# A residual made feature by feature early, turned to token order later, and read back in large loads

## The chip, the core and the metric

One core of one Trainium2 chip runs the whole program. The metric is the device time of one execution in microseconds. The engines are TensorE (PE; PEld is its weight load), VectorE (DVE), ScalarE (ACT), GpSimd (POOL) and SyncE (SP); here SP and POOL only issue DMAs. Each engine works through its own queue in order. On chip there are SBUF (128 partitions) and PSUM; `dram` tensors lie in device memory.

## What is computed

Two transformer-like blocks in a row, for 512 tokens of 2048 features. The first ends in a norm whose output x1 is both the input of the second and the residual of its first half:

```python
def first_block(x, p, ...):
    hn = rmsnorm(h, norm_gain[i])
    ...
    h = h + concatenate([ya, yb]) @ w_out[i]
    h = h + (p[i] @ w_ple[i]) * sigmoid(h @ w_ple_gate[i])
    return rmsnorm(h, final_gain)                       # x1

def second_block(x, c, positions, ...):                 # x is x1
    mod = silu(c) @ w_ada[l] + b_ada[l]
    sh_a, sc_a, gt_a, sh_f, sc_f, gt_f = split(mod, 6)
    h = rmsnorm_2(x, g_pre_attn[l]) * (1.0 + sc_a) + sh_a
    qa, ka, va, qb, kb, vb = split(h @ w_in[l], 6)
    ...                                                 # dilated and differential attention
    x = x + gt_a * rmsnorm_2(mix @ w_out[l], g_post_attn[l])
    h = rmsnorm_2(x, g_pre_ffn[l]) * (1.0 + sc_f) + sh_f
    f = (silu(h @ w_gate[l]) * (h @ w_up[l])) @ w_down[l]
    return x + gt_f * rmsnorm_2(f, g_post_ffn[l])
```

## The kernel before

**The matmuls.** Every large product is three matmuls on float32 split into a high and a low part: high by high, high by low, low by high. A weight piece (256 rows by 512 columns, 512 KB) is loaded by SP into `raw` (four buffers, up to six pieces ahead); up to three pieces ahead ScalarE copies the high half (`whi`) and VectorE subtracts it for the low half (`wlo`, L185). A gemm goes over the pieces; the order of TensorE's instructions is written by hand, while the queues of the other engines are put in order by a scheduler.

**Side work.** `side(steps, ticks, least=1)` (L120) gives a list of small steps to the program, and `tick()`, called once per k step of every gemm (12 matmuls in a full one), issues some of each list: `len(steps) / ticks`, but at least `least`. `finish` issues what is left of a list. `self.ada` is such side work: the adaLN product `silu(c) @ w_ada` on VectorE, tile after tile of `w_ada` (`wa`, 512 KB, SP), two multiply-adds (`ada`) for each.

**The pools.** The large pool `t4` has 30 buffers of 4 KB a partition; in it lie the split operands (16 tiles), the eight tiles `h2` of the first block's output, the attention's `qk` and `v`, the `wa` tiles, and later `mo`. The small pool `t2` has 8 buffers of 2 KB a partition for everything that passes by.

**x1.** `attention()` (L1203) starts with q and k of the first batch, then gives x1 as side work (L1238): 14 empty steps and 16 steps at half a step a tick. A step `x1(f)` (L1212) is, for a block of 128 features: on VectorE the product `x1 = h2 * final_gain * rxrow` (`rxrow` is the row of 1/rms, L1214; the trace prints the tile as `x`), on VectorE a transpose in blocks of 32 x 32 into `x1t` (L1217), and four DMAs on POOL into `x1d`, in device memory, in token order (L1219). The eight `h2` tiles stay until their last product. After q and k of a batch ScalarE copies the four PSUM tiles into fresh `qk` tiles (`project`, L1067).

**w_out2.** (L1267) The output projection runs with tokens on the partitions; its results go to `mo` tiles. The second half of the tokens of the later feature groups is computed while the first half is finished, and a first part of the feed-forward products (`up`) while the second half is. What finishes a half is `chain(hf)` (L1321), side work again: a load of the residual for three units ahead (`xr`, 256 KB, POOL, L1294), the root of the norm, then for eight units (4 groups of 512 features x 2 blocks of 128 tokens) the sum `mo = mo * root + xr` on VectorE (L1296), its square on ScalarE and a write to `x2d`, then the next load; then the second root, the normed tiles `xn`, their transposes on TensorE (`turn`, L1313) and the modulated operand `M` for the feed-forward products. `until` is a hook of a gemm that issues steps of the chain until the operand for its k is there.

Of the kernel before, what the change touches and what calls it, by code (L numbers as in the profile page):

```python
# [14 lines left out]
MUL, ADD, SUB, MAX = ALU.mult, ALU.add, ALU.subtract, ALU.max  # L15

P = 128
S = 512
D = 2048
KT = D // P  # L20
# [19 lines left out]
class Kernel:  # L40
# [1162 lines left out]
    def attention(self):  # L1203
        nc = self.nc
        cosA, sinA, cosB, sinB = self.tab[:4]
        self.mixd, self.x1d = self.dram("mixd", [D, S]), self.dram("x1d", [S, D])
        self.order = [b * 4 + h + (8 if kind == "b" else 0) for kind, b in self.BATCHES for h in range(4)]
        self.M = [None] * KT
        self.keep = False
        x, fg = self.H, self.cols["final_gain"]  # L1210

        def x1(f):  # L1212
            t = self.t2("x1")
            self.stt(t, self.h2[f], fg[:, f:f + 1], self.rxrow, MUL, MUL)  # L1214

            u = self.t2("x1t")
            nc.vector.transpose(u, t)  # L1217
            for b in range(4):
                nc.gpsimd.dma_start(self.x1d[:, f * P + b * 32:f * P + b * 32 + 32].rearrange("(c p) i -> p c i", p=32),  # L1219
                                  u[b * 32:b * 32 + 32, :].rearrange("p (c i) -> p c i", i=32))  # L1220

        def load(f):
            t = self.t2("ml")
            nc.sync.dma_start(t, self.mixd[f * P:(f + 1) * P, :])
            self.M[f] = self.pair("M")
            self.split(self.M[f], t)

        s = self.side(self.norm_steps(self.norm1(1), 1), 32)
        q, k = self.qk(), self.qk()
        for hf in range(2):  # L1230
            cs = slice(hf * 256, hf * 256 + 256)
            for o in (q, k):
                ps = self.gemm(x, half=hf)
                for i in range(4):
                    nc.scalar.copy(o[i][:, cs], ps[i][:, cs])
            if hf == 0:
                self.finish(s)
        self.side([None] * 14 + [lambda f=f: x1(f) for f in range(KT)], 60, 0)  # L1238
        self.adas = self.side(self.ada(12, 20), 165, 0)
        s = None  # L1240
        for n, (kind, b) in enumerate(self.BATCHES):
            t = (cosB, sinB, 32) if kind == "b" else (cosA, sinA, 64)
            if n == 3:
                break
            if n == 0:
                self.side(self.rope(q, *t) + self.rope(k, *t), 10)
            else:
                q, r = self.project(x, *t)
                self.side(r, 10)
                k, r = self.project(x, *t)  # L1250
                self.side(r, 10)
            v = self.values(x)
            if s:
                self.finish(s)
            s = self.side(self.attn_steps(kind, b, range(4), q, k, v), (47, 47, 31)[n])
        v = self.values(x)
        qk, r = self.project(x, *t)
        self.finish(s)
        self.keep = True
        self.side([None] * 2 + [lambda f=f: load(f) for f in self.order[:12]], 14)  # L1260
        s = self.side(r + self.attn_steps(kind, b, (0, 1), qk[:2], qk[2:], v), 16)
        qk, r = self.project(x, *t)
        self.finish(s)
        self.side(r + [None] * 6 + self.attn_steps(kind, b, (2, 3), [0, 0] + qk[:2], [0, 0] + qk[2:], v), 13)
        self.modding = self.H = None

    def w_out2(self):  # L1267

        nc, tc = self.nc, self.tc
# [6 lines left out]
        x = [[self.t4("mo", [P, 2, S]) for _ in range(2)] for _ in range(4)]  # L1276
# [5 lines left out]
        def evict(g, ps, b0):  # L1282
            for i, p in enumerate(ps):
                self.act(self.t2("sq"), p, AF.Square, accum_out=ss[:, 0, b0 + i, g:g + 1])
                self.tt(mo(b0 + i, g), p, corow[g], MUL)

        def root(n, b0, st):
            v = self.small("w2s", 2, 2)
            nc.vector.tensor_reduce(v, ss[:, n, b0:b0 + 2], axis=mybir.AxisListType.X, op=ADD)
            st[n] = self.rsq(v, 2)  # L1290

        def load(b, g, st):
            st[b, g] = self.t2("xr")
            nc.gpsimd.dma_start(st[b, g], self.x1d[b * P:(b + 1) * P, g * S:(g + 1) * S])  # L1294

        def add(b, g, st):  # L1296
            o = mo(b, g)
            self.stt(o, o, st[0][:, b % 2:b % 2 + 1], st.pop((b, g)), MUL, ADD)
            self.act(self.t2("sq"), o, AF.Square, accum_out=ss[:, 1, b, g:g + 1])
            nc.gpsimd.dma_start(self.x2d[b * P:(b + 1) * P, g * S:(g + 1) * S], o)  # L1300

        def normed(g, b0, st):
            st["n", g] = [self.t2("xn") for _ in range(2)]
            for i in range(2):
                self.ts(st["n", g][i], mo(b0 + i, g), st[1][:, i:i + 1], MUL)

        def turn(g, st):

            n = st.pop(("n", g))
            st["t"] = [self.aux("turn") for _ in range(2)]  # L1310
            for i in range(4):
                for b in range(2):
                    nc.tensor.transpose(st["t"][i // 2][:, (i % 2 * 2 + b) * P:(i % 2 * 2 + b + 1) * P],  # L1313
                                        n[b][:, i * P:i * P + P], self.ident)

        def mod(k, hf, st):
            i = k % 4
            self.mod_step(k, hf, st["t"][i // 2][:, i % 2 * 256:i % 2 * 256 + 256])
            st["done"] = k

        def chain(hf):  # L1321
            b0, st = 2 * hf, {"done": -1}
            units = [(b0 + i, g) for g in range(4) for i in range(2)]
            steps = [lambda: [load(*u, st) for u in units[:3]], None, lambda: root(0, b0, st), None]
            for n, u in enumerate(units):
                steps.append(lambda n=n, u=u: (add(*u, st), n < 5 and load(*units[n + 3], st)))
            steps += [None, lambda: root(1, b0, st), None, lambda: normed(0, b0, st), None, None, None]
            for g in range(4):
                steps += [lambda g=g: (turn(g, st), g < 3 and normed(g + 1, b0, st)), None]
                steps += [lambda k=k: mod(k, hf, st) for k in range(4 * g, 4 * g + 4)]  # L1330
            s = self.side(steps, len(steps))

            def until(k):
                while st["done"] < k:
                    f = s[0].pop(0)
                    if f:
                        f()
            return until

        for g in range(4):  # L1340
            evict(g, self.gemm(M, tok=True, half=None if g < 2 else 0), 0)
        self.finish(self.adas)
        F = self.M
        self.mod_begin(F, None, None, ("g_pre_ffn_2",), 3)
        self.us = [self.dram(f"us{n}", [256, S]) for n in range(self.NU)]

        def halves():
            for hf in range(2):
                hook = chain(hf)
                for n in range(2):  # L1350
                    if hf == 0:
                        evict(n + 2, self.gemm(M, tok=True, half=1), 2)
                    else:
                        self.up(n, self.gemm(F, half=0, hook=hook0 if n == 0 else None), slice(0, 256))
                hook0 = hook
            self.low.close()
            self.F, self.M = F, None
            if self.NS < self.NU:
                self.sp = self.ctx.enter_context(tc.tile_pool(name="sp", bufs=1, reuse_waits="tile"))
                self.C = [None] * 8  # L1360
                self.side([None] * 10 + [x for k in range(4) for x in (lambda k=k: self.sums(k), *[None] * 4)], 32)
            for n in range(2):
                self.up(n, self.gemm(F, half=1, hook=hook if n == 0 else None), slice(256, S))

        halves()
        for n in range(2, self.NS):
            hook = None
            if n == self.NS - 1 < self.NU - 1:
                hook = lambda k: self.sums(k // 2 + 1) if k in (6, 8, 10, 12) else None
            self.up(n, self.gemm(F, hook=hook))  # L1370

# [9 lines left out]
    def sums(self, k):  # L1381


        nc = self.nc
        A, B = self.F[k], self.F[k + 8]
        x, y = self.t2("sa"), self.t2("sb")
# [326 lines left out]
```

## Time and profile before

| | us |
|---|---|
| runs before: median of 3 (lowest, highest) | 3197.99 (3195.05, 3198.09) |
| the profiled execution's own time | 3195.01 |
| span of its profile | 3193.3 |
| TensorE matmuls busy | 3122.3 (98% of the span) |
| VectorE busy | 2357.3 (74%) |
| ScalarE busy | 1333.5 (42%) |
| GpSimd busy | 126.7 (4%) |

The mean clock that TensorE was granted in the profiled execution is 0.994 of full speed. The span is that of the instructions; the execution's time is 1.7 us more. TensorE's load of weights runs beside its matmuls and is not in the first number.

### The profile page before, as it was taken

To read this page: it belongs to the slowest core of one execution; us is meant where nothing else is said; L and a number is where in the kernel's file an instruction comes from. 1 tells how busy PE (TensorE), PEld (TensorE's weight loads), DVE (VectorE), ACT (ScalarE), POOL (GpSimd) and SP (SyncE) were. 2 spreads that over 40 slices of the span, in tenths; PEclk is the share of its full clock that TensorE was granted. 3 is DMA by queue.
4 is the path that set the end of the run, shared out by engine and by line. 5 is a ranking of instruction groups with operands and counts; after the bars stand their busy time and mean duration, and the time that the engine had idled before them with its cause. 6 is when DMAs were issued, how large, how long until landed. Compare 5 with 4: busy or idle time off the path is not lost. (4 is left out here: it accounts for less than half of the span.)

```text
span 3193.3 us, 50279 instructions
## 1 busy us (share of the span) xinstructions
PE 3122.3 (98%) x18484; PEld 2741.0 (86%) x18484; DVE 2357.3 (74%) x4638; ACT 1333.5 (42%) x2056; POOL 126.7 (4%) x217
## 2 busy tenths in 40 slices
PE   8999999999999899999899899999999999999998
PEld 7887878888899777788787899999999999888887
DVE  9787777866897587876745787888888888864445
ACT  6333443222466344433534653443334434333433
POOL 0010000000000021000001100000000000000000
PEclk9999999999999999999999999999999999999999
DMA  5763746755556365443426754444444445965664
GB/s 187 214 207 122 234 153 213 257 157 188 185 173 217 112 182 149 147 157 127 128 75 198 222 162 113 119 120 117 119 118 119 120 117 162 361 200 157 186 210 152
DMA packets 399624, 531.33 MB, mean 166 GB/s; under 512 B 43424, under 2 KB 222752, under 8 KB 399376
## 3 DMA queue, kind: packets, MB, share of 16 engines
q1 hardware_dynamic: 384448, 490.45, 49.0%
q0 software_dynamic: 10576, 29.70, 3.3%
q10 hardware_dynamic: 4352, 7.96, 0.7%
q8 instruction: 145, 2.38, 0.3%
q14 instruction: 103, 0.84, 0.1%
HBM read 491.34 MB, written 36.63 MB: 165 GB/s over the span
## 5 line engine op out<-in xcount | busy, mean ns | idle before, releaser
L185 DVE TENSOR_TENSOR wlo<-raw,whi 128x1024 fp32r<-128x1024 f32 (+1 forms) x655 | 756.2, 1160 | 478.9 <-ACT whi L261 390.4
L261 ACT CAST whi<-raw 128x1024 fp32r<-128x1024 f32 (+1 forms) x407 | 441.7, 1086 | 796.5 <-PE mm L315 344.0
L315 PE MATMUL mm<-H,whi 128*128 128x512 f32 (+1 forms) x2048 | 516.7, 344 | 12.9 <-ACT qk L1067 10.6
L1554 PE MATMUL mm<-whi,u 128*128 128x512 f32 x1344 | 415.0, 390 | 0.2 <-DVE u L185 0.2
L315 PEld LDWEIGHTS mm<-H,whi 128*128 128x128 f32 x2048 | 349.1, 192 | 57.6 <-ACT qk L1067 11.0
L315 PE MATMUL mm<-H,wlo 128*128 128x512 f32 (+1 forms) x1024 | 347.3, 339 | 1.5 <-DVE wlo L185 1.5
L315 PE MATMUL mm<-X,whi 128*128 128x512 f32 x1024 | 322.6, 396 | 8.4 <-ACT whi L261 6.7
L279 ACT CAST whi<-raw 128x1024 fp32r<-128x1024 f32 x152 | 159.7, 1051 | 400.5 <-issue 242.8
L194 DVE SCALAR_TENSOR_TENSOR ada<-wa,siluc,ada 128x512 f32<-128x512 f32 x360 | 268.8, 747 | 43.2 <-DMA wa<-in_w_ada_dram 38.2
L1554 PEld LDWEIGHTS mm<-whi,u 128*128 128x128 f32 x1344 | 251.7, 188 | 52.8 <-DVE u L185 0.6
L1554 PE MATMUL mm<-wlo,u 128*128 128x512 f32 x672 | 261.5, 389 | 0.0
L1444 PE MATMUL mm<-s,thi 128*128 128x256 f32 x1216 | 232.0, 283 | 0.0
L1444 PE MATMUL mm<-M,whi 128*128 128x256 f32 x1216 | 231.9, 283 | 0.0
L315 PEld LDWEIGHTS mm<-X,whi 128*128 128x128 f32 x1024 | 189.2, 189 | 48.8 <-ACT whi L261 6.7
L315 PEld LDWEIGHTS mm<-H,wlo 128*128 128x128 f32 x1024 | 195.9, 191 | 23.4 <-DVE wlo L185 1.7
L315 PE MATMUL mm<-X,wlo 128*128 128x512 f32 x512 | 201.3, 393 | 3.0 <-DVE wlo L185 3.0
L1444 PEld LDWEIGHTS mm<-M,whi 128*128 128x128 f32 x1216 | 189.8, 192 | 0.1
L1444 PEld LDWEIGHTS mm<-s,thi 128*128 128x128 f32 x1216 | 189.7, 192 | 0.0
L1444 PE MATMUL mm<-M,wlo 128*128 128x256 f32 x608 | 172.1, 283 | 0.0
L1444 PE MATMUL mm<-s,tlo 128*128 128x256 f32 x608 | 172.1, 283 | 0.0
L313 PE MATMUL mm<-whi,H 128*128 128x512 f32 x512 | 162.6, 399 | 0.0
L313 PE MATMUL mm<-whi,M 128*128 128x512 f32 x512 | 160.8, 395 | 1.3 <-ACT qk L1067 1.3
(390 smaller groups left out, 6016.3 us busy)
## 6 DMA issues: line engine op xcount, KB each, us to landing
wa<-in_w_ada_dram SPq DMA_DIRECT2D x192, 512.0 KB, 6.0
raw<-in_w_in_dram SPq DMA_DIRECT2D x111, 512.0 KB, 3.9
raw<-in_w_down_dram SPq DMA_DIRECT2D x88, 512.0 KB, 4.2
raw<-in_w_out_dram SPq DMA_DIRECT2D x80, 512.0 KB, 4.2
ur<-us SPq DMA_DIRECT2D x140, 256.0 KB, 4.6
raw<-in_w_in_dram SPq DMA_DIRECT2D x130, 256.0 KB, 3.1
raw<-in_w_ple_gate_dram SPq DMA_DIRECT2D x48, 512.0 KB, 4.0
raw<-in_w_gate_dram SPq DMA_DIRECT2D x152, 128.0 KB, 2.1
```

What stands on the lines that cost most here:

```text
L185: self.nc.vector.tensor_tensor(o, x, y, op=op)
L194: self.nc.vector.scalar_tensor_tensor(o, x, s, y, op0=op0, op1=op1)
L261: nc.scalar.copy(h, r)
L279: nc.scalar.copy(hv, v)
L313: nc.tensor.matmul(ps[i], x[k][:, xi, c], wt[:, a, :], **fl)
L315: nc.tensor.matmul(ps[i][:, cs], wt[:, a, c], x[k][:, xi, cs], **fl)
L1444: nc.tensor.matmul(ps[j][:, s], wt[:, s, slot], self.C[k][j][xi], start=(k == 0 and s == 0 and i == 0), stop=(k == 7 and s == 1 and i == 2))
L1554: nc.tensor.matmul(ps[b], u[a][:, xi, b * P:(b + 1) * P], wt[:, a, :], start=(n == a == j == 0), stop=(n == NU - 1 and a == 1 and j == 2))
```

## The change

Three pieces of code are changed. In `attention`, `x1(f)` makes the product only and has SP write it to a new tensor `x1f` in device memory, features by tokens; the 16 steps come at one a tick, with no empty steps ahead. A second list, `self.x1s`, does the rest later: after 44 empty steps, for each of the 16 blocks `back(f)` (SP loads the block from `x1f` into a small tile), one empty step, `turn(f)` (the transpose and the four DMAs on POOL as before) and four empty steps, one step a tick. It is finished after the first feature group of `w_out2`. In `w_out2` the loads of a unit are replaced by `load(b0)`: four loads of 512 KB (two feature groups each) into the large pool, issued for the first half ahead of `mod_begin`, and for the second half at the end of the first half's eight sums. The chain's lists keep their length.

```diff
+        self.x1f = self.dram("x1f", [D, S])
+        turned = {}
+
         def x1(f):
             t = self.t2("x1")
             self.stt(t, self.h2[f], fg[:, f:f + 1], self.rxrow, MUL, MUL)
+            nc.sync.dma_start(self.x1f[f * P:(f + 1) * P, :], t)
+
+        def back(f):
+            turned[f] = self.t2("x1")
+            nc.sync.dma_start(turned[f], self.x1f[f * P:(f + 1) * P, :])
+
+        def turn(f):
 
             u = self.t2("x1t")
-            nc.vector.transpose(u, t)
+            nc.vector.transpose(u, turned.pop(f))
...
-        self.side([None] * 14 + [lambda f=f: x1(f) for f in range(KT)], 60, 0)
+        self.side([lambda f=f: x1(f) for f in range(KT)], 40)
+        self.x1s = self.side([None] * 44 + [x for f in range(KT) for x in (lambda f=f: back(f), None, lambda f=f: turn(f),
+                                                                          *[None] * 4)], 156)
...
-        def load(b, g, st):
-            st[b, g] = self.t2("xr")
-            nc.gpsimd.dma_start(st[b, g], self.x1d[b * P:(b + 1) * P, g * S:(g + 1) * S])
+        x1s = {}
+
+        def load(b0):
+            x1 = x1s[b0] = [[self.t4("xr", [P, 2, S]) for _ in range(2)] for _ in range(2)]
+            for g in range(2):
+                for b in range(2):
+                    tc.keep_in_program_order(
+                        nc.gpsimd.dma_start(x1[b][g].rearrange("p g n -> p (g n)"),
+                                            self.x1d[(b0 + b) * P:(b0 + b + 1) * P, g * 1024:g * 1024 + 1024]))
 
         def add(b, g, st):
             o = mo(b, g)
-            self.stt(o, o, st[0][:, b % 2:b % 2 + 1], st.pop((b, g)), MUL, ADD)
+            self.stt(o, o, st[0][:, b % 2:b % 2 + 1], x1s[b & 2][b % 2][g // 2][:, g % 2], MUL, ADD)
...
-            steps = [lambda: [load(*u, st) for u in units[:3]], None, lambda: root(0, b0, st), None]
-            for n, u in enumerate(units):
-                steps.append(lambda n=n, u=u: (add(*u, st), n < 5 and load(*units[n + 3], st)))
-            steps += [None, lambda: root(1, b0, st), None, lambda: normed(0, b0, st), None, None, None]
+            steps = [None, None, lambda: root(0, b0, st), None] + [lambda u=u: add(*u, st) for u in units]
+            steps += [lambda: hf == 0 and load(2), lambda: root(1, b0, st), None, lambda: normed(0, b0, st), None, None, None]
...
             evict(g, self.gemm(M, tok=True, half=None if g < 2 else 0), 0)
+            if g == 0:
+                self.finish(self.x1s)
         self.finish(self.adas)
+        load(0)
```

The change moves instructions on the engines that a scheduler puts in order; TensorE's order stays as it is. Three places, in each the queue before and the queue now. The numbers behind a name tell one tile from another.

ScalarE's queue in the attention, at the copies of a projection's results into `qk`, with what each instruction waits for (DMAHW and DMASW are DMAs of the hardware and the software queues). Before:

```order
L258 CAST whi_10185<-raw_9946 128x512 [waits DMAHW7_49,DMAHW6_49,PE_49]
L258 CAST whi_10185<-raw_9946 128x512
L1149 COPY pT_10170<-turn_10166 128x384 [waits PE_49]
L1067 COPY qk_10172<-mm_9593 128x512 [waits DMAHW5_49,DMAHW1_49,DVE_49]
L1067 COPY qk_10172<-mm_9594 128x512
L1067 COPY qk_10173<-mm_9595 128x512 [waits DMAHW6_49,DMAHW2_49,DVE_49]
L1067 COPY qk_10173<-mm_9596 128x512
```

Now:

```order
L197 ACTIVATE oq_10139,ss_9904<-mix_10136 128x128 [waits DVE_49]
L1067 COPY qk_10205<-mm_9642 128x512 [waits PE_49]
L197 ACTIVATE p_10169,den_9903<-p_10169,m_10170 128x512 [waits DVE_49,Activation_49]
L197 ACTIVATE p_10174,d_1684_10162<-p_10174,m_10175 128x512 [waits DVE_49,Activation_49]
L1067 COPY qk_10205<-mm_9643 128x512 [waits PE_49]
L1067 COPY qk_10206<-mm_9644 128x512 [waits PE_49]
L1149 COPY pT_10203<-turn_10199 128x384 [waits PE_49,Activation_49]
L1067 COPY qk_10206<-mm_9645 128x512
```

The copies waited for two loads and for VectorE beside what is done already; now they wait for TensorE, and two softmax steps (`p`) stand between them.

SP's queue in the attention, around the first load back of x1. Before:

```order
L227 DMA raw_10603<-in_w_in_dram 128x2x512
L227 DMA raw_10675<-in_w_in_dram 128x2x512
L940 DMA wa_10792<-in_w_ada_dram 128x2x512
L227 DMA raw_10750<-in_w_in_dram 128x2x512
L227 DMA raw_10840<-in_w_in_dram 128x2x512
L940 DMA wa_10978<-in_w_ada_dram 128x2x512
L940 DMA wa_11063<-in_w_ada_dram 128x2x512
```

Now:

```order
L227 DMA raw_10596<-in_w_in_dram 128x2x512
L227 DMA raw_10660<-in_w_in_dram 128x2x512
L1222 DMA x_1798_10678<-x1f 128x512
L227 DMA raw_10729<-in_w_in_dram 128x2x512
L227 DMA raw_10817<-in_w_in_dram 128x2x512
L940 DMA wa_10941<-in_w_ada_dram 128x2x512
L940 DMA wa_11024<-in_w_ada_dram 128x2x512
L227 DMA raw_10891<-in_w_in_dram 128x2x512
```

A load from `x1f` stands between the weight loads; the other 15 follow further on in the same way, among `raw`, `wa` and `mixd` transfers.

VectorE's queue in `w_out2`, at the sums of the first half. Before:

```order
L194 SCALAR_TENSOR_TENSOR mo_14559<-mo_14559,rsy_15745,xr_15717 128x512
L194 SCALAR_TENSOR_TENSOR mo_14561<-mo_14561,rsy_15745,xr_15719 128x512
L194 SCALAR_TENSOR_TENSOR mo_14559<-mo_14559,rsy_15745,xr_15721 128x512
L185 TENSOR_TENSOR wlo_15799<-raw_15705,whi_15798 128x1024
L194 SCALAR_TENSOR_TENSOR mo_14561<-mo_14561,rsy_15745,xr_15782 128x512
L185 TENSOR_TENSOR wlo_15829<-raw_15729,whi_15828 128x1024
L194 SCALAR_TENSOR_TENSOR mo_14560<-mo_14560,rsy_15745,xr_15794 128x512
L185 TENSOR_TENSOR wlo_15857<-raw_15766,whi_15856 128x1024
L194 SCALAR_TENSOR_TENSOR mo_14562<-mo_14562,rsy_15745,xr_15812 128x512
L194 SCALAR_TENSOR_TENSOR mo_14560<-mo_14560,rsy_15745,xr_15824 128x512
L185 TENSOR_TENSOR wlo_15883<-raw_15796,whi_15882 128x1024
L194 SCALAR_TENSOR_TENSOR mo_14562<-mo_14562,rsy_15745,xr_15842 128x512
```

Now:

```order
L194 SCALAR_TENSOR_TENSOR mo_14608<-mo_14608,rsy_15796,xr_15727 128x512
L194 SCALAR_TENSOR_TENSOR mo_14610<-mo_14610,rsy_15796,xr_15729 128x512
L194 SCALAR_TENSOR_TENSOR mo_14608<-mo_14608,rsy_15796,xr_15727 128x512
L185 TENSOR_TENSOR wlo_15846<-raw_15762,whi_15845 128x1024
L194 SCALAR_TENSOR_TENSOR mo_14610<-mo_14610,rsy_15796,xr_15729 128x512
L194 SCALAR_TENSOR_TENSOR mo_14609<-mo_14609,rsy_15796,xr_15728 128x512
L185 TENSOR_TENSOR wlo_15872<-raw_15780,whi_15871 128x1024
L194 SCALAR_TENSOR_TENSOR mo_14611<-mo_14611,rsy_15796,xr_15730 128x512
L194 SCALAR_TENSOR_TENSOR mo_14609<-mo_14609,rsy_15796,xr_15728 128x512
L194 SCALAR_TENSOR_TENSOR mo_14611<-mo_14611,rsy_15796,xr_15730 128x512
```

Eight sums before used eight tiles `xr` of one load each, with four `wlo` among them; now two sums share a load, and two `wlo` stand among them.

## Rows read from the trace of the kernel before

**Rows 1.** The page, part 1: engines, busy us (share), instructions.

```profile
PE 3122.3 (98%) x18484; PEld 2741.0 (86%) x18484; DVE 2357.3 (74%) x4638; ACT 1333.5 (42%) x2056; POOL 126.7 (4%) x217
```

**Rows 2.** Windows of 40 us: stretch, length, busy us (x instructions) per engine, PEclk, DMA share, GB/s.

```profile
1040.00:1080.00 40.00, 40.00 (x191) 31.50 (x189) 18.02 (x57) 17.12 (x41) 0.00 (x0) 1.00 0.28 89
1080.00:1120.00 40.00, 29.39 (x152) 22.73 (x148) 28.67 (x95) 13.38 (x38) 5.84 (x9) 0.92 0.50 147
1160.00:1200.00 40.00, 38.90 (x197) 30.39 (x196) 36.05 (x115) 19.08 (x45) 15.22 (x24) 1.00 0.70 199
1200.00:1240.00 40.00, 37.99 (x182) 30.98 (x181) 32.90 (x74) 19.65 (x36) 10.50 (x17) 1.00 0.54 144
1800.00:1840.00 40.00, 32.84 (x252) 31.86 (x251) 25.59 (x52) 24.50 (x41) 3.79 (x7) 0.91 0.61 194
```

**Rows 3.** Waits of TensorE, 1000 to 1280 us: us in total, times, longest.

```profile
PE mm L315 <- ACT qk L1067: 10.6, 1, 10.6
PE logits L1100 <- ACT oq L197: 2.9, 1, 2.9
```

**Rows 4.** Timeline at 1110 to 1120: start, length, instruction, [idle before <-releaser].

```profile
1110.47 0.75 DVE L194 SCALAR_TENSOR_TENSOR ada<-wa,siluc,ada 128x512 f32<-128x512 f32 x1 [2.98 <-DMA wa<-in_w_ada_dram]
...
1116.64 0.74 DVE L194 SCALAR_TENSOR_TENSOR x<-h,vecs,rxrow 128x512 f32<-128x512 f32 x1
...
1117.97 0.70 DVE L1217 STREAM_TRANSPOSE x1t<-x 128x512 f32<-128x512 f32 x1
...
1119.34 1.07 ACT L1067 COPY qk<-mm 128x512 f32<-128x512 f32 x2 [9.00 <-DVE ada L194]
...
1119.97 1.22 PE L315 MATMUL mm<-H,whi 128*128 128x512 f32 x2 [10.61 <-ACT qk L1067]
```

**Rows 5.** Windows of 4 us, columns as in rows 2.

```profile
1118.00:1122.00 4.00, 2.03 (x5) 1.64 (x6) 2.84 (x6) 2.15 (x4) 2.56 (x4) 0.50 0.84 266
1122.00:1126.00 4.00, 4.00 (x18) 3.29 (x17) 1.80 (x3) 0.37 (x2) 0.04 (x1) 0.78 0.40 74
1150.00:1154.00 4.00, 4.00 (x10) 3.13 (x10) 2.89 (x9) 0.00 (x0) 0.00 (x0) 0.50 0.54 150
1816.00:1820.00 4.00, 3.74 (x17) 3.74 (x18) 0.93 (x3) 0.35 (x1) 1.08 (x2) 0.50 0.59 197
```

**Rows 6.** Waits of TensorE, 1720 to 1830 us, in `w_out2`.

```profile
PE mm L313 <- DVE wlo L185: 3.2, 2, 2.4
PE mm L315 <- ACT u L197: 2.4, 1, 2.4
PE mm L315 <- DVE u L185: 2.3, 1, 2.3
PE mm L315 <- DVE M L185: 1.6, 1, 1.6
PE turn L1313 <- DVE xn L189: 1.6, 1, 1.6
PE mm L315 <- DVE wlo L185: 0.8, 1, 0.8
```

**Rows 7.** The tile `xr`: the sums that read it, and their waits (us, times).

```profile
L194 DVE SCALAR_TENSOR_TENSOR mo<-mo,rsy,xr x16: 743/750/753, 1738.7 to 1807.2; 128x512 f32<-128x512 f32 x16
...
  DMA xr<-x1d: 15.6, 8
```

**Rows 8.** DMA issues: operation, count, KB each, median us to landing.

```profile
xr<-x1d POOLq DMA_DIRECT2D x16, 256.0 KB, 5.7
...
x<-x2d SPq DMA_DIRECT2D x8, 512.0 KB, 6.1
...
ml<-mixd SPq DMA_DIRECT2D x12, 256.0 KB, 4.3
```

**Rows 9.** The tile `x1t`: duration ns min/median/max, first and last start.

```profile
L1217 DVE STREAM_TRANSPOSE x1t<-x x16: 695/706/714, 1096.1 to 1223.1; 128x512 f32<-128x512 f32 x16
```

**Rows 10.** Timeline of ScalarE ahead of `u`.

```profile
1810.97 1.28 ACT L197 ACT_TABLE_LOAD   x1
```

More of the change, by code (lines that the diff above doesn't have):

```diff
@@ L1214, in x1 @@
             self.stt(t, self.h2[f], fg[:, f:f + 1], self.rxrow, MUL, MUL)
+            nc.sync.dma_start(self.x1f[f * P:(f + 1) * P, :], t)
[3 more added lines that the diff above has]
+        def turn(f):
             u = self.t2("x1t")
-            nc.vector.transpose(u, t)
+            nc.vector.transpose(u, turned.pop(f))
             for b in range(4):
                 nc.gpsimd.dma_start(self.x1d[:, f * P + b * 32:f * P + b * 32 + 32].rearrange("(c p) i -> p c i", p=32),
-                                  u[b * 32:b * 32 + 32, :].rearrange("p (c i) -> p c i", i=32))
+                                    u[b * 32:b * 32 + 32, :].rearrange("p (c i) -> p c i", i=32))
         def load(f):
```

## Prediction

> **What bounds the kernel now.** The first view is the busy shares of the engines: TensorE's matmuls fill 3122.3 us of the span of 3193.3 [rows 1], so 71 us are left in which TensorE stands, and the order of its instructions does not change. An edit elsewhere can win only from those 71 us and from matmuls that run at the lower of the two clock levels. The second view, windows of 40 us, shows where both lie around the code that changes: between 1080 and 1120 us TensorE stands 10.6 us at a granted clock of 0.92, between 1800 and 1840 it stands 7.2 us at 0.91, while in the stretch just ahead, 1040 to 1080, it never stands and VectorE is busy for 18.02 us of 40 [rows 2]. The third view, who waited for whom on TensorE, names the causes. In the attention one wait for ScalarE's copy `qk` (L1067) takes 10.6 us and one for `oq` 2.9 [rows 3]; in `w_out2` seven waits take 11.9 us [rows 6].
>
> The timeline explains the large one. ScalarE's copy into the new `qk` tile starts only at 1119.34, after 9.00 us of idleness that an `ada` step of VectorE ended, and TensorE goes on 0.6 us later [rows 4]. Why would a copy out of PSUM wait for an `ada` step? The `qk` tile takes a buffer of the large pool (30 buffers) which a `wa` tile held, and VectorE reads that tile last; the order of the kernel before writes the same wait on the copy. VectorE has a queue there: it had waited 2.98 us for the load of `wa` and then runs adaLN steps, x1's product and x1's transpose, 0.7 us each, in program order [rows 4]. The pool is tight because the eight tiles `h2` (the first block's output) live until x1 is made of them, and x1 comes one of 16 feature blocks per two ticks, transposed from 1096 to 1223 us [rows 9].
>
> The other place, in `w_out2`, is simpler: VectorE's sums `mo` stand 15.6 us in 8 waits for the loads of `xr` [rows 7], which are issued three units ahead and take 5.7 us to land [rows 8]. VectorE is in order, so the weight halves `wlo`, the normed tile `xn`, `M` and `u` behind those sums are late, and TensorE waits for each of them [rows 6].
>
> **What the change does, and its price.**
>
> *The large stall.* x1's 16 products (0.74 us each [rows 4]) now run one per tick, ahead of the second batch; in VectorE's order all stand 70 rows or more ahead of the place where the first stood before, in the stretch in which VectorE was busy less than half the time. 16 x 0.74 = 12 us more there against 22 us of idle [rows 2]: I cost it at nothing, under TensorE's cover; without that cover it would be 12 us. With them the eight `h2` buffers come free, and `wa` tiles go there. In the order of the changed kernel the copies into `qk` wait for TensorE alone. So the 10.6 us go, and with them the slow matmuls behind: TensorE restarted at a granted clock of 0.50, the lower of its levels of 1.2 and 2.4 GHz (2.03 us of work up to 1122, worth 1.0) and 0.78 (4.00 us, worth 0.9) [rows 5], against 1.00 elsewhere. Together 12.5 us.
>
> *The rest of that stretch.* The wait of 2.9 us for `oq` [rows 3] and the 4.00 us at half clock that follow (worth 2.0) [rows 5] come from ScalarE's own queue and VectorE's lateness together; the transposes (16 x 706 ns, 11.3 us) leave VectorE in that stretch, where it was busiest [rows 9]. I take half of 4.9: 2.5 us. Between 1160 and 1240 TensorE stands 3.1 us in small waits [rows 2]; half again: 1.5. Bounds of the two together: 0 and 8.0.
>
> *The sums of `w_out2`.* Four loads of 512 KB stand ahead of each half. A load of that size took 6.1 us to land (`x<-x2d`), one of 256 KB 5.7 [rows 8]. The first four are issued right after the block's last adaLN piece, at about the time of the first `xr` loads before; the other four follow the last sum of the first half. The sums run from 1738.7 to 1807.2 in two groups [rows 7], so both sets have far longer than 6 us to land, and no sum waits for them. In the first half TensorE then loses its waits for `wlo` (3.2) and `xn` (1.6): 4.8. In the second half those for `wlo` (0.8) and `M` (1.6) go: 2.4. The two at the handover, `u` of ScalarE and of VectorE (2.4 and 2.3), come of the same lag: about half of the 15.6 us [rows 7] fall into this half. But a new table load of 1.28 us stands ahead of `u` on ScalarE whatever VectorE does [rows 10], so I leave 1.5 of the 4.7 and take 3.2. The matmuls behind ran 3.74 us at 0.50 [rows 5]: 1.9. Sum 12.3; bounds 4.8 (the first half alone) and 13.8 (all of it).
>
> Against joining loads speaks a rule of the Trainium skill, Perfetto Trace Analysis, section DMA Optimizations: splitting a DMA may let some of the work start sooner. By it the first sum of a half would stand until a whole 512 KB had landed. That would cost at most the 0.4 us between the two landings, and nothing where the load is early; the sum stays as it is.
>
> *New traffic.* SP issues 16 more writes (to `x1f`) and 16 more loads (back into SBUF), each 256 KB, between the weight loads. The nearest row: a load of that size and kind from the same queue (`ml`) landed in 4.3 us [rows 8]. Each write waits for a product that VectorE runs ahead of the `wlo` that frees the next weight buffer, so the loads behind it are not held. Each load back stands two ticks ahead of its transpose. A tick is 12 matmuls; 191 in 40.00 us make that 2.5 us [rows 2], so there are 5.0 us for 4.3. That is a thin margin, and SP's queue adds to it where a `raw` or `wa` load waits for its buffer. When the transpose waits, so do `wlo` and the attention's steps behind it on VectorE. In `w_out2`, 15.6 us of such waiting on VectorE cost TensorE 9.5 (all its waits for VectorE there, 3.2 + 2.3 + 1.6 + 1.6 + 0.8): 0.61 for one [rows 6, 7]. I choose half of the 16 loads 0.4 us late, a tenth of a landing: 8 x 0.4 x 0.61 = 2 us. Ends: 0, and 42 (16 x 4.3 x 0.61, a whole landing each time). I am near the low end because weight halves are made three pieces ahead, six ticks or 15 us.
>
> A second rule speaks against the round trip: the Trainium skill, DMA: Bandwidth & Descriptors, section Issuing engines are not separate DMA queues, says that transfers of every engine share the same 16 DMA engines. By it the 8.4 MB could slow `wa` and `raw`; the trace has a share of 0.28 to 0.70 in these stretches [rows 2], so there is room in each on average, and I add no term.
>
> POOL issues the same 64 transposed pieces, only spread out, and 8 loads for 16; nobody waits for its queue.
>
> **Sum.** 12.5 + 2.5 + 1.5 + 12.3 - 2 = 26.8, about 27 us. The profiled execution took 3195.0, so 3168 on its scale. The median of the three runs is 3198.0, 3 us above it; the forecast of a median is **3171 us**, 0.8% less.
>
> **Rivals.**
>
> 1. *The loads of `w_out2` don't become early.* The four tiles are the large pool's, and that pool is full there: 16 tiles of the second block's operand, 8 `mo`, 4 + 4 `xr` are 32 against 30. The second half's loads must wait for the first half's tiles. For: the count. Against: they are issued behind the last sum of the first half anyway, when its tiles are free, and the second half's first sum is a whole gemm away. It gives 4.8 instead of 12.3: 19 us, 3179. Chance 0.12.
>
> 2. *The large stall only moves.* Eight `ada` steps still stand close together in VectorE's order at that place, and if their loads are as late as before (2.98 us [rows 4]) the softmax steps behind them are late, and TensorE stands at the next `logits` or `turn` instead. For: the waits named `oq` and `turn` follow close behind already [rows 3]. Against: with eight buffers more, `wa` loads are issued earlier. The 12.5, 2.5 and 1.5 shrink to about 2: 12 us in all, 3186. Chance 0.13.
>
> 3. *Slower: the loads back stop VectorE.* SP works in order; a load back that queues behind a weight load waiting for its buffer lands after its transpose is due, VectorE stands, `wlo` slips, TensorE waits and restarts at half clock. The gains are 26.8 + 2 = 28.8; at 0.61 they are used up when VectorE stands 47 us in all, 2.9 per load; at 4.3 per load the result is 28.8 - 42 = 13 us slower, 3211. For: the margin of 0.7 us. Against: three pieces of lead, and VectorE was busy 18 to 36 of 40 us in the stretches shown [rows 2], so it can catch up between two loads. Chance 0.07. The shared engines of the second rule would act through this same wait.
>
> 4. *Nothing comes of it.* The order's waits are not the times: another tile of the large pool may hold `qk` back, and the sums may stand for ScalarE instead. Gains and costs cancel: 3195 to 3201. Chance 0.08.
>
> The forecast's own case has 0.60.
>
> **How the numbers follow.** Best case of the bounds: 12.5 + 8.0 + 13.8 = 34, 3164, and a run as fast as the fastest of before lies 3 lower, 3161. I set the range from 3158 to 3189, which takes in rivals 1 and 2 and leaves out 3, 4 and some tails, under 2 in 10. A measurement of this kernel can tell about 0.2%, 6.4 us, from no change. Faster by more than that: the forecast's case, rival 1 and most of rival 2, 0.84. Same 0.09, slower 0.07.
>
> **What would show it.** In the profile after: no wait of TensorE for `qk` L1067 above 1 us near 1110, the granted clock 1.00 there; VectorE busier from 1040 to 1080; no wait of `mo` for `xr`, and TensorE's waits in `w_out2` down from 11.9 to about 2; landings of `x<-x1f` near 4.3 us and few waits of `x1t` for them. Wrong: a new wait for `oq`, `logits` or `turn` of 5 us or more at 1110 to 1130 (rival 2), `x1t` waiting 2.9 us or more for each load (rival 3), `mo` still waiting for `xr` in the second half (rival 1).

## The result, and the profile after

| | us |
|---|---|
| changed kernel: median of 4 (lowest, highest) | 3159.61 (3158.48, 3162.62) |
| kernel before, 4 runs | 3196.52 (3193.18, 3198.09) |
| ratio, 95% interval | 0.9887 (0.987 to 0.9905) |
| profiled executions: before, after | 3195.01, 3162.62 |

The medians differ by 36.9 us; 3171 had been forecast, with a range of 3158 to 3189. The forecast was on the right side and inside the range, and it asked for too little: 27 us against 37. The gain is also above the 34 us that the prediction gave as its best case; the time lies inside the range only because the lower end was set 6 us below that case.

The page of the changed kernel begins:

```profile
span 3160.9 us, 50349 instructions
PE 3115.3 (99%) x18484; PEld 2737.2 (87%) x18484; DVE 2355.8 (75%) x4638; ACT 1333.5 (42%) x2056; POOL 121.9 (4%) x209
```

TensorE is busy 7 us less than before [rows 1], with the same instructions, and the span is 32.4 us shorter, so most of the gain is time in which it stood. The windows that answer to [rows 2] (same columns):

```profile
1040.00:1080.00 40.00, 39.24 (x183) 30.77 (x182) 23.46 (x62) 15.18 (x36) 0.00 (x0) 1.00 0.49 161
1080.00:1120.00 40.00, 40.00 (x206) 31.43 (x204) 22.92 (x92) 18.55 (x51) 0.00 (x0) 1.00 0.37 119
1160.00:1200.00 40.00, 39.90 (x205) 31.94 (x205) 30.06 (x87) 25.76 (x52) 5.21 (x8) 1.00 0.56 179
1200.00:1240.00 40.00, 39.02 (x184) 30.82 (x184) 29.20 (x80) 12.79 (x26) 5.18 (x8) 1.00 0.65 200
1800.00:1840.00 40.00, 40.00 (x336) 39.81 (x335) 30.01 (x49) 28.09 (x47) 2.17 (x4) 1.00 0.56 175
```

The two stretches that stood out are full: 1080 to 1120 went from 29.39 to 40.00, 1800 to 1840 from 32.84 to 40.00, both at a granted clock of 1.00. All of TensorE's waits of 0.3 us or more from 1040 to 1240 us and from 1690 to 1850 us are now:

```profile
PE turn L1147 <- DVE p L194: 1.0, 2, 0.6
PE logits L1100 <- DVE m L1108: 0.8, 2, 0.6
PE logits L1100 <- ACT oq L197: 0.3, 1, 0.3
```

```profile
PE mm L315 <- ACT u L197: 2.4, 1, 2.4
```

The waits for `qk` (10.6) and of 2.9 for `oq` [rows 3] are gone or down to 0.3, and of the seven waits in `w_out2` [rows 6] one is left, ScalarE's `u`. ScalarE's copies into `qk`, which answer to [rows 4], no longer wait for VectorE:

```profile
1110.90 0.59 ACT L1067 COPY qk<-mm 128x512 f32<-128x512 f32 x1 [1.94 <-PE mm L315]
...
1112.91 1.05 ACT L1067 COPY qk<-mm 128x512 f32<-128x512 f32 x2
```

GpSimd's queue shows the loads of `xr`. The first four leave some 170 us ahead of the first sum (1719.99), the other four right after the first half's last write and 34 us ahead of the second half's first sum (1765.35); no sum waits for one of them:

```profile
1548.97 0.57 POOL L1311 DMA_DIRECT2D xr<-x1d  x1 [18.41 <-ACT oq L197]
1553.07 0.55 POOL L1311 DMA_DIRECT2D xr<-x1d  x1 [3.53 <-ACT M L200]
1555.77 0.53 POOL L1311 DMA_DIRECT2D xr<-x1d  x1 [2.14 <-PE mm L315]
1558.50 0.53 POOL L1311 DMA_DIRECT2D xr<-x1d  x1 [2.20 <-PE mm L315]
...
1721.03 1.87 POOL L1318 DMA_DIRECT2D x2d<-mo  x3 [162.00 <-DVE mo L194]
...
1728.55 1.74 POOL L1311 DMA_DIRECT2D xr<-x1d  x3
1730.51 0.53 POOL L1311 DMA_DIRECT2D xr<-x1d  x1 [0.21 <-issue]
```

The transposes stand where the timing of the second list puts them, a load back lands in 3.5 us, and a load of 512 KB in 6.7 (columns as in [rows 8, 9]):

```profile
L1227 DVE STREAM_TRANSPOSE x1t<-x x16: 700/704/714, 1166.3 to 1527.0; 128x512 f32<-128x512 f32 x16
```

```profile
x<-x1f SPq DMA_DIRECT2D x16, 256.0 KB, 3.5
...
xr<-x1d POOLq DMA_DIRECT2D x8, 512.0 KB, 6.7
```

**Where the time went.** TensorE's order is the same in both kernels, so the start of the same instruction can be compared in the two traces. The table gives that difference at a few of them, and the step since the one above:

| instruction of TensorE | before | after | difference | step |
|---|---|---|---|---|
| first `fin` after 570 | 573.29 | 575.29 | +2.00 | +2.00 |
| first `logits` after 1050 | 1054.99 | 1058.53 | +3.54 | +1.54 |
| last `mm` ahead of the large stall | 1108.97 | 1113.55 | +4.58 | +1.04 |
| `mix`, behind the large stall | 1123.87 | 1115.85 | -8.02 | -12.60 |
| `turn` | 1163.15 | 1148.75 | -14.40 | -6.38 |
| `turn` | 1376.11 | 1357.94 | -18.17 | -3.77 |
| `mix` | 1559.78 | 1541.16 | -18.62 | -0.45 |
| `turn` of the first half, second group | 1772.89 | 1748.28 | -24.61 | -5.99 |
| `turn` of the second half | 1822.70 | 1790.78 | -31.92 | -7.31 |
| `fin` | 2754.40 | 2722.02 | -32.38 | -0.46 |

The first line lies ahead of everything the change touches, and the second holds a wait of 1.41 us for `wlo` at 997.88 that four other kernels with the same code there (below) don't have. The third is a price of the change that comes back: VectorE now runs `ada` steps between 1040 and 1080, and TensorE waits 0.18 us for a softmax step at 1059.63 and 0.58 at 1063.86. Such waits, 0.75 to 2.4 us together, stand there in all nine kernels in which two or more `h2` buffers come free early, and in none of the other four. From the large stall on the steps sum up to 37.0 us: attention gave 22.8 of it, `w_out2` 13.3. The two traces differ by 32.4 us in all, as the profiled execution of the changed kernel was the slowest of its four.

### The profile page after: what moved, and what is told of

Same layout as the page of the kernel before. It is cut to its first block, busy times and chain, and to the rows that moved or that the text cites. A ratio compares the mean times of both kernels' runs of the same rounds, so it can differ in the third digit from the quotient of the medians.

```text
span 3160.9 us, 50349 instructions
## 1 busy us (share of the span) xinstructions
PE 3115.3 (99%) x18484; PEld 2737.2 (87%) x18484; DVE 2355.8 (75%) x4638; ACT 1333.5 (42%) x2056; POOL 121.9 (4%) x209
## 5 line engine op out<-in xcount | busy, mean ns | idle before, releaser
L185 DVE TENSOR_TENSOR wlo<-raw,whi 128x1024 fp32r<-128x1024 f32 (+1 forms) x655 | 756.0, 1160 | 466.4 <-ACT whi L261 373.9
L279 ACT CAST whi<-raw 128x1024 fp32r<-128x1024 f32 x152 | 159.6, 1050 | 400.7 <-issue 247.5
```

The source lines that it names most:

```text
L185: self.nc.vector.tensor_tensor(o, x, y, op=op)
L279: nc.scalar.copy(hv, v)
```

## The experiments

Two questions. In the attention: is it the buffers of `h2` that come free early, or VectorE, which is relieved of 16 products and 16 transposes just there? In `w_out2`: is it the size of the loads, their place in the program, or that they no longer stand behind the sums in GpSimd's queue?

### One part alone

The first kernel has x1's part of the change and the old loads:

```diff
-        x1s = {}
-
-        def load(b0):
...
+        def load(b, g, st):
+            st[b, g] = self.t2("xr")
+            nc.gpsimd.dma_start(st[b, g], self.x1d[b * P:(b + 1) * P, g * S:(g + 1) * S])
...
-        load(0)
```

> Only x1's part of the change: products early, written to x1f, turned later; the residual comes in 16 loads of 256 KB as before. If the two parts are independent, this keeps what the trace of the changed kernel shows up to the first turn of w_out2 (about 19 us earlier there, of which 12.7 around the large stall) and loses the 13 us of w_out2: about 3177, with 15 us of waits of mo for xr. If the gain of w_out2 came from x1's part (x1d written in another place, a lighter VectorE), it stays near 3163.

Measured: 3172.4 us, some 5 us less than guessed, ratio to the kernel before 0.9933 (0.992 to 0.9945). The sums wait as before [rows 7]:

```profile
DVE mo L194 <- DMA xr<-x1d: 16.9, 8, 5.5
```

The second has the loads alone (x1 as in the kernel before).

> Only the four large loads per half; x1 is made and transposed in one step as before. Independent parts: the wait of 10.6 us for qk and those behind it stay, w_out2 wins its 13 us: about 3184, no waits of mo for xr. If the loads only pay because x1d is complete earlier or the pool is freer, less than 6 us are won.

Measured: 3183.18 us, ratio 0.9958 (0.9945 to 0.997). By the table's method the stretch of the sums, from 1600 to the second half's `turn`, gives 13.2 us in its trace, and the large wait is there:

```profile
PE mm L315 <- ACT qk L1067: 10.1, 1, 10.1
```

The product of the two ratios, 0.9933 x 0.9958 = 0.9891, is that of the whole change, 0.9887, within the intervals. No interaction of the two parts shows.

### Are they the buffers?

The changed kernel, but the last 8 of the 512 columns of each product are made at the old ticks, so that each `h2` tile is held as long as before. VectorE's work in the stretch stays small:

```diff
         def x1(f):
             t = self.t2("x1")
-            self.stt(t, self.h2[f], fg[:, f:f + 1], self.rxrow, MUL, MUL)
-            nc.sync.dma_start(self.x1f[f * P:(f + 1) * P, :], t)
+            self.stt(t[:, :504], self.h2[f][:, :504], fg[:, f:f + 1], self.rxrow[:, :504], MUL, MUL)
+            nc.sync.dma_start(self.x1f[f * P:(f + 1) * P, :504], t[:, :504])
+
+        def late(f):
+            t = self.t2("x1")
+            self.stt(t[:, 504:], self.h2[f][:, 504:], fg[:, f:f + 1], self.rxrow[:, 504:], MUL, MUL)
+            nc.gpsimd.dma_start(self.x1f[f * P:(f + 1) * P, 504:], t[:, 504:])
...
+        self.side([None] * 14 + [lambda f=f: late(f) for f in range(KT)], 60, 0)
```

> The changed kernel, but the last 8 of 512 columns of each x1 block are made at the old ticks and written to x1f by POOL, so that each h2 tile is held as long as before, while VectorE's load in that stretch is as light as in the changed kernel (16 products of 8 columns). Theory of the buffers: the copies into qk wait for the wa tiles again, the wait near 10 us and the half clock behind it are back, 3172 or more. Theory of VectorE's load: the waits stay away or shrink to under 3 us, 3160 to 3164.

Measured: 3177.48 us (0.9946, 0.9934 to 0.9959), 18 us more than the changed kernel. TensorE's waits from 1000 to 1280 us begin:

```profile
PE mm L315 <- ACT qk L1067: 11.0, 1, 11.0
PE logits L1100 <- ACT oq L197: 2.9, 1, 2.9
```

The line that decides is the sum of four windows from 1080 to 1240 us (160 us; then busy us of each engine). The kernel before, the changed kernel, and this one:

```profile
sum 160.00, PE 143.38 PEld 113.30 DVE 128.35 ACT 73.84 POOL 41.22; mean PE 35.85 PEld 28.32 DVE 32.09 ACT 18.46 POOL 10.30
```

```profile
sum 160.00, PE 158.65 PEld 125.44 DVE 119.39 ACT 82.23 POOL 10.39; mean PE 39.66 PEld 31.36 DVE 29.85 ACT 20.56 POOL 2.60
```

```profile
sum 160.00, PE 143.29 PEld 113.22 DVE 113.26 ACT 72.66 POOL 16.57; mean PE 35.82 PEld 28.30 DVE 28.31 ACT 18.16 POOL 4.14
```

VectorE is busy 15 us less here than in the kernel before, 113.3 against 128.4 us, and TensorE works 143.3 us as before, not 158.7. Relieving VectorE of x1 wins nothing that this trace shows: from `logits` to the last `mix` of the table it gains 2.0 us, where the kernel with the loads alone, whose attention is that of before, gains 2.7 and the changed kernel 22.2. By the medians this kernel is 5.7 us below the one with the loads alone, with intervals that overlap, so a few us for VectorE are not excluded. The late products themselves are not what costs: of the kernels below, the one with seven tiles held has 14 of the 16 and no wait for `qk`.

### What the buffers are for

SP's queue shows whom they serve. In the kernel before SP issues 15 weight loads from 1054 on and the next `wa` load only at 1105; in the changed kernel six `wa` loads leave between 1053 and 1061; with all `h2` held the first of that stretch leaves at 1108:

```profile
1054.56 50.46 SPq L227 DMA_DIRECT2D raw<-in_w_in_dram  x15
1105.32 1.39 SPq L940 DMA_DIRECT2D wa<-in_w_ada_dram  x3
```

```profile
1053.16 0.97 SPq L940 DMA_DIRECT2D wa<-in_w_ada_dram  x2
...
1059.03 2.00 SPq L940 DMA_DIRECT2D wa<-in_w_ada_dram  x4
```

```profile
1108.31 1.49 SPq L940 DMA_DIRECT2D wa<-in_w_ada_dram  x3
```

So six adaLN tiles come some 50 us earlier, and VectorE works on them from 1040 to 1080, where no `ada` step read a `wa` tile in the kernel before; with all `h2` held none does either. In the changed kernel:

```profile
L194 DVE SCALAR_TENSOR_TENSOR ada<-wa,siluc,ada 128x512 f32<-128x512 f32 x12 | 9.0, 746 | 2.3 <-DMA wa<-in_w_ada_dram 2.2
```

In the kernel before the tiles came at the moment in which `qk` needed two buffers, and `qk` got the ones that the last of them had: ScalarE had to wait until VectorE had read them [rows 4].

How many buffers does that take? Three kernels hold the last four, six or seven of the eight tiles:

```diff
-        self.side([None] * 14 + [lambda f=f: late(f) for f in range(KT)], 60, 0)
+        self.side([None] * 14 + [(lambda f=f: late(f)) if f >= 8 else None for f in range(KT)], 60, 0)
```

(8 is 4 for six tiles and 2 for seven, and `x1` makes all 512 columns of the others.)

> As the run with all eight h2 tiles held, but only the last four are; the other four come free early. If the copy into qk needs just one or two free buffers, the wait of 10 us stays away and so do the smaller waits behind it: 3158 to 3164. If all eight buffers are in use by then (by wa tiles that fill what is free), part of the 18 us comes back: 3165 to 3172. If the smaller waits (oq 2.9, turn, mix) come of buffers of their own and not of the large wait, they come back without it: about 3165.

> The last six held, two free early: the copies into qk wait for the landing of a wa tile in the queue's order, not for VectorE. If one or two buffers are enough, 3158 to 3166 with no wait of qk over 2 us; if the dose counts, the wait is between that of four held and that of all held.

> Seven held, one free early: qk needs two buffers, and one of them must come from elsewhere. Between the run with six held and that with eight (11.0 us of wait, 3177): 3166 to 3175. If it equals eight, the two buffers that qk takes are all that counts; if it equals six, one is enough.

| `h2` tiles held | us, median | ratio to before (interval) | wait for `qk` |
|---|---|---|---|
| none (the change) | 3159.61 | 0.9887 (0.987 to 0.9905) | none |
| four | 3161.22 | 0.9896 (0.9881 to 0.9911) | none |
| six | 3164.59 | 0.9908 (0.9893 to 0.9923) | none |
| seven | 3167.91 | 0.9918 (0.9901 to 0.9934) | none |
| eight | 3177.48 | 0.9946 (0.9934 to 0.9959) | 11.0 |

The guess of 3166 to 3175 for seven held the time, but not the reason: with a single buffer free early the wait for `qk` is gone altogether. Which two buffers `qk` then took is not shown. The `wa` loads use the free one in turn, one after the other, from 1049 on:

```profile
1049.00 0.46 SPq L940 DMA_DIRECT2D wa<-in_w_ada_dram  x1
...
1057.17 0.37 SPq L940 DMA_DIRECT2D wa<-in_w_ada_dram  x1
...
1062.57 0.37 SPq L940 DMA_DIRECT2D wa<-in_w_ada_dram  x1
...
1069.18 6.65 SPq L940 DMA_DIRECT2D wa<-in_w_ada_dram  x2
...
1080.71 0.37 SPq L940 DMA_DIRECT2D wa<-in_w_ada_dram  x1
```

What comes back with seven held are waits behind it, 2.7 of the 2.9 us for `oq` among them:

```profile
PE logits L1100 <- ACT oq L197: 2.7, 1, 2.7
PE turn L1147 <- DVE p L194: 2.0, 2, 1.6
```

So one free buffer ends the large wait, and the smaller ones do not go with it: they take more buffers. The wait for `oq` is 0.8 us with two free and 0.3 with four; and with four free the time can't be told from that of the changed kernel. The medians rise step by step, though neighbours among the first four lines are not told apart by their intervals.

### Is the way through x1f needed?

Product, transpose and writes at the early ticks, straight from the tile; no `x1f`:

```diff
         def x1(f):
             t = self.t2("x1")
             self.stt(t, self.h2[f], fg[:, f:f + 1], self.rxrow, MUL, MUL)
-            nc.sync.dma_start(self.x1f[f * P:(f + 1) * P, :], t)
...
             u = self.t2("x1t")
-            nc.vector.transpose(u, turned.pop(f))
+            nc.vector.transpose(u, t)
...
-        self.x1s = self.side([None] * 44 + [x for f in range(KT) for x in (lambda f=f: back(f), None, lambda f=f: turn(f),
-                                                                          *[None] * 4)], 156)
```

> Product, transpose and the four DMAs of x1 all at the early ticks, straight from the tile, without x1f; the large loads as in the changed kernel. If what counts is that the h2 buffers come free early, the wait for qk is gone here as well and the time is that of the changed kernel, plus what 11 us more of VectorE between 990 and 1040 cost in waits for wlo there (0 to 6 us): 3160 to 3168. If what counts is that VectorE is lighter between 1040 and 1240, also that is so here. If the round trip through x1f costs TensorE more than it seems, this kernel is faster than the changed one by over 2 us.

Measured: 3162.36 us (0.9893, 0.9878 to 0.9909). That is no different from the changed kernel. The transposes ran from 957 to 1045 us, ahead of the crowded place:

```profile
L1217 DVE STREAM_TRANSPOSE x1t<-x x16: 704/710/715, 957.5 to 1044.9; 128x512 f32<-128x512 f32 x16
```

The way through `x1f` costs nothing that shows, and wins nothing either.

One more run delays the 16 products by ten ticks (`[None] * 10` ahead of them, 26 ticks for the list).

> The changed kernel with ten empty ticks ahead of the 16 products. If the 2.6 us that TensorE loses between 924 and 1060 us in the changed kernel come of the products standing among the wlo and the rotation of q and k there, they are won: about 3157. If they come of chance or of the writes to x1f, the time stays at 3160. The buffers still come free before 1080, so the wait for qk stays away in both.

Measured: 3158.48 us (0.9888, 0.9873 to 0.9903). The wait for `wlo` near 998 is gone in its trace, but in its place `turn` waits 1.65 us at 1060. As the wait at 998 is missing also in kernels with unchanged code there, this settles nothing; the medians differ by 1.1 us. (The 2.6 us of that text compare two different `logits` of the two traces; at the same one it is 1.5, the second step of the table.)

### The loads of w_out2

Three kernels change one thing each. The four loads of a half at the first step of its own chain:

```diff
-            steps = [None, None, lambda: root(0, b0, st), None] + [lambda u=u: add(*u, st) for u in units]
-            steps += [lambda: hf == 0 and load(2), lambda: root(1, b0, st), None, lambda: normed(0, b0, st), None, None, None]
+            steps = [lambda: load(b0), None, lambda: root(0, b0, st), None] + [lambda u=u: add(*u, st) for u in units]
+            steps += [None, lambda: root(1, b0, st), None, lambda: normed(0, b0, st), None, None, None]
...
-        load(0)
```

> The changed kernel with each half's four loads given at the first step of its own chain, four steps ahead of its sums, instead of a gemm earlier. Theory: what matters is that in POOL's queue no load stands behind a sum of its own half, since POOL has nothing else to do and issues as soon as a buffer is free; then the loads are still tens of us ahead and nothing is lost, 3158 to 3163. Rival, the earlier place in the program is what pays: the first sums of each half wait some 6 us, 3 to 8 us are lost, 3163 to 3168.

Measured: 3161.37 us (0.9898, 0.9883 to 0.9912), no wait of `mo` for `xr`. The loads leave at the same times as in the changed kernel (first at 1548, last at 1731): GpSimd issues them as early from either place, so a place a gemm earlier in the program is not needed.

Each load split in two of 256 KB (`h` is 0 and 1), in the same place:

```diff
-                        nc.gpsimd.dma_start(x1[b][g].rearrange("p g n -> p (g n)"),
-                                            self.x1d[(b0 + b) * P:(b0 + b + 1) * P, g * 1024:g * 1024 + 1024]))
+                            nc.gpsimd.dma_start(x1[b][g][:, h],
+                                                self.x1d[(b0 + b) * P:(b0 + b + 1) * P, g * 1024 + h * S:g * 1024 + h * S + S]))
```

> The changed kernel with every load of 512 KB split in two of 256 KB into the same tiles, at the same places. If the size does not matter, only that the loads stand ahead of the sums, the time is that of the changed kernel, 3158 to 3163, no wait of mo for xr. If larger loads are what pays, waits of mo come back and 3 us or more are lost.

Measured: 3161.2 us (0.9895, 0.9881 to 0.991), no wait either: the size doesn't matter.

Large loads, but `load` gives only the two of the first two feature groups, and the other two are issued behind the half's second sum:

```diff
-            steps = [None, None, lambda: root(0, b0, st), None] + [lambda u=u: add(*u, st) for u in units]
+            steps = [None, None, lambda: root(0, b0, st), None] + [lambda n=n, u=u: (add(*u, st), n == 1 and load(b0, 1)) for n, u in enumerate(units)]
```

> The changed kernel with two of the four loads of each half issued ahead of the sums and the other two behind the second sum, as the kernel before chained its loads to the sums; size as in the changed kernel. Theory of the chained issue: the fifth sum of each half waits 3 to 5 us for a load that is issued 2 sums ahead, TensorE loses 1 to 3 us in each half: 3162 to 3167. Theory of the size: no loss, 3158 to 3162.

Measured: 3166.15 us (0.9913, 0.9897 to 0.993), some 6 us more than the changed kernel; the intervals overlap, but its four runs (from 3164.43) lie above all runs of the changed kernel and of the two kernels before this one. GpSimd issues the second two loads of each half among the writes, and VectorE waits for them:

```profile
1720.02 1.07 POOL L1311 DMA_DIRECT2D xr<-x1d  x2
...
1766.38 1.07 POOL L1311 DMA_DIRECT2D xr<-x1d  x2
```

```profile
1726.12 1.41 DVE L194 SCALAR_TENSOR_TENSOR mo<-mo,rsy,xr 128x512 f32<-128x512 f32 x2 [3.27 <-DMA xr<-x1d]
...
1772.68 0.75 DVE L194 SCALAR_TENSOR_TENSOR mo<-mo,rsy,xr 128x512 f32<-128x512 f32 x1 [4.29 <-DMA xr<-x1d]
```

TensorE's waits from 1690 to 1850 us:

```profile
PE mm L315 <- ACT u L197: 3.3, 1, 3.3
PE mm L315 <- DVE u L185: 2.0, 1, 2.0
PE mm L315 <- DVE wlo L185: 0.2, 1, 0.2
```

By the table's method this kernel loses 5.9 us in the second half and nothing in the first, though VectorE waited 3.27 us there. It is the chaining that cost. In the kernel before, GpSimd's queue reads like this:

```profile
1747.57 0.55 POOL L1300 DMA_DIRECT2D x2d<-mo  x1 [4.58 <-DVE mo L194]
1748.11 0.54 POOL L1294 DMA_DIRECT2D xr<-x1d  x1
```

A load stands behind the write of a sum, which stands behind a load that was itself behind a sum: "three units ahead" in the program was one landing per three sums.

## Why the prediction was right, and too small

- **The large stall, 12.5 us.** Right: 12.60, and by the mechanism that was named. The runs with tiles held show that it is the buffers.
- **The products, at nothing.** The size was about right, the place was not. They were covered with idle time of VectorE from 1040 to 1080; they ran earlier, from 956 to 1033, where VectorE was fuller, and their one sign is the wait of 1.41 us at 997.88 in a single trace. That VectorE became busier from 1040 to 1080 (18.02 to 23.46 us) came true for another reason, the `ada` steps, and these cost most of the 1.04 us of the table's third line, for which the sum had no term.
- **The rest of that stretch, 2.5 + 1.5 us.** This step failed. It was laid half to VectorE's lateness, since the transposes leave there, and half to ScalarE's queue, and so half of it was taken. It gave 6.38 + 3.77 = 10.2 us, 9.3 of it up to 1240, where the prediction's stretch ends: more than the upper bound of 8.0. With the tiles held and VectorE lighter 1.9 of it is won, no more than in the kernel with the loads alone (2.1), so what the change won there belongs to the buffers too; and as the seven-held kernel shows, it takes more of them than the large stall does. The term was halved by a guess, and the bound counted waits that the profile lists and one window of the clock only; the wait for `oq`, those of `turn` and `mix` and the stretch at half clock from 1150 all went. Some of it is chance, as the last section shows for that stretch.
- **The sums, 12.3 us.** Right: 5.99 + 7.31 = 13.3. The prediction left 1.5 us of the handover for a table load; the wait for ScalarE's `u` still takes 2.4 us, as before, while the one for VectorE's `u` and the slow matmuls behind it are gone. The reason given, that the loads have far longer than their landing, is right; the place that was given for it is not what counts (the run with late loads), but the queue. The first loads were also placed too late: they left at 1549, not at about the time of the first `xr` loads before, which is 1686.4.
- **The rule against joining loads.** The Trainium skill, Perfetto Trace Analysis, section DMA Optimizations, says that splitting may let some start sooner. Here split and joined loads took 3161.2 and 3159.6 us, no difference, as both are far ahead of their use.
- **New traffic, -2 us.** Too dear. No transpose shows a wait for its load back, and the kernel without the round trip is no faster. Loads back landed in 3.5 us where 4.3 had been taken from the nearest row. That all transfers share the same DMA engines (the Trainium skill, DMA: Bandwidth & Descriptors, section Issuing engines are not separate DMA queues) had no price that shows: in two stretches with loads back, 1160 to 1200 and 1200 to 1240, the share went from 0.70 to 0.56 and from 0.54 to 0.65, and `wa` from 6.0 us to land to 6.2. The rise from 0.28 to 0.49 between 1040 and 1080 is not this traffic, as none of it leaves from 1034 to 1156 (columns as in [rows 9]):

```profile
L1218 SPq DMA_DIRECT2D x1f<-x x16: 320/339/843, 956.8 to 1033.8; - x16
L1222 SPq DMA_DIRECT2D x<-x1f x16: 338/339/447, 1156.5 to 1516.5; - x16
```

- **The rivals.** The full large pool (1) did not show: the second half's loads left 34 us ahead of its first sum. The stall that only moves (2) did not either, since the `wa` loads came 50 us earlier, which the prediction had held against it; what moved is about 1 us, to 1060. VectorE stopped by the loads back (3), and nothing at all (4), fell.
- **The size.** Of the 9 us by which the table's steps from `logits` on exceed the sum, 6.2 are the halved term, 2 the traffic and 1 the sums. That the time still lies inside the range is luck: it owes this to the margin for fast runs, not to a term.

## What to carry to other kernels

A wait of a copy out of PSUM for an unrelated engine was here a wait for a buffer: look who held it last, and then who starves while the pool is full. One tile released early was enough here to end the large wait, since a stream of loads could run ahead of the crowded place; the waits behind it were a matter of the same buffers, but went only as more of them came free, so price them by the buffers that they need and not as a share by guess. Work that is let ahead has a price where it lands, here about 1 us. Loads that stood in an in-order queue behind work that depends on earlier loads were not ahead of anything here, however many units ahead the program asks for them; give them a place in front of that work. Their size, 256 or 512 KB, then made no difference here.

## What the runs showed of the hardware

The same wait was not always followed by the same clock. At 473 us, ahead of all the code that differs, TensorE waits 2.2 us for `sg` in all thirteen traces; in the kernel before and three others it went on at a granted clock of 1.00, in the other nine it stood between 0.63 and 0.96, on the mean of the four microseconds from 476 to 480. Before and after (columns as in [rows 2]):

```profile
476.00:480.00 4.00, 4.00 (x19) 3.33 (x18) 4.00 (x8) 1.62 (x2) 0.00 (x0) 1.00 0.31 92
```

```profile
476.00:480.00 4.00, 4.00 (x17) 3.23 (x16) 3.03 (x6) 1.67 (x2) 0.00 (x0) 0.87 0.30 96
```

The slow microseconds are 1.6 of the 2.0 us of the table's first line. In the same way the stretch behind the wait of 2.9 us for `oq` ran at half clock in the kernel before [rows 5] and at 1.00 in the kernel with the loads alone. Differences of up to 2 us between two single traces can thus be chance in this kernel, and a gain counted from a stretch at half clock behind a short wait is one that some executions never had to lose.
